# Average pooling over a 537 MB array: loads of 48 KB per partition on one DMA queue and stores of 48 KB on another, in place of 64 KB loads and 32 KB stores on one queue

## The chip, the cores and the metric

The kernel runs on one core of a Trainium2 chip. The core has a VectorE (DVE in the profile), a ScalarE (ACT), a TensorE (PE), a GpSimd (POOL) and a SyncE (SP), an on-chip memory of 128 partitions, and 16 DMA engines that move data between it and the main memory (HBM). DMAs are started by instructions on an engine's instruction stream; those of SP go into SP's DMA queue, those of ACT into ACT's. One DMA over 128 partitions is spread over the 16 engines, eight partitions each.

The metric is the device time of one execution in microseconds, the median of several runs.

## The reference

The input x is 64 x 256 x 8192 in float32; the pooling window and the stride are both 4.

```python
def reference(x: np.ndarray, kernel_size: int, stride: int) -> np.ndarray:
    batch, channels, length = x.shape
    out_len = (length - kernel_size) // stride + 1
    output = np.zeros((batch, channels, out_len), dtype=np.float32)
    for i in range(out_len):
        start = i * stride
        output[:, :, i] = np.mean(x[:, :, start : start + kernel_size], axis=2)
    return output
```

Every four neighbours along the last axis become their mean. Since 8192 is a multiple of 4 and no window crosses a row, the whole array can be read as one flat run of 134,217,728 numbers, each four of which give one output. 536.87 MB are read and 134.22 MB are written.

## The kernel before

The flat array is cut into 32 groups, and a group into 128 contiguous runs of 32,768 numbers (`run`, 128 KB), one for each partition. A group is loaded in two loads (`PER_STORE`), each with 16,384 numbers (`LOAD`, 64 KB) of every partition: 63 full loads, and the last one is cut in two pieces (`LAST`, 11,264 and 5,120 numbers). A tile `xt` holds one load; there are two of them. A tile `ot` holds the results of a whole group, 8,192 numbers (32 KB) per partition; there are two of them as well.

`pool` works on one load. VectorE adds neighbours in pairs, in place (line 51: 16,384 numbers become 8,192), and adds neighbours of the result in pairs into `ot` (line 56: 8,192 become 4,096). ScalarE multiplies these by 0.25 in place (line 57).

All DMAs are issued by SP, in the order of the program: the load of step n (line 70), and behind the second load of a group the store of the group before (line 74). A load waits until VectorE has read the tile that it overwrites, that is until line 56 of step n-2 is done; the store waits for line 57 of its group's second load. So the DMA queue holds load, load, store, load, load, store, one after the other. At the end, behind the two pieces of the last load, stand the store of group 30 (line 74), the store of the first half of group 31 (line 76) and one store for each piece (line 81).

Of the kernel before, what the change touches and what calls it, by code (L numbers as in the profile page):

```python
# [1 line left out]

# [4 lines left out]

ADD = mybir.AluOpType.add

LOAD = 16384  # L10
PER_STORE = 2
LAST = (11264, 5120)


@with_exitstack
def kernel(
    ctx: ExitStack,
    tc: tile.TileContext,
    x: bass.AP,
    kernel_size: bass.AP,  # L20
    stride: bass.AP,
    out: bass.AP,
):

    nc = tc.nc
    K = int(kernel_size)
    assert K == 4 and int(stride) == 4 and x.shape[-1] % 4 == 0
    P = nc.NUM_PARTITIONS  # L30
    dt = x.dtype
    inv_k = 1.0 / K

    run = LOAD * PER_STORE
    total = x.shape[0] * x.shape[1] * x.shape[2]
    groups = total // (P * run)
    assert groups * P * run == total and groups >= 2
    xg = x.flatten_outer_dims().rearrange("r l -> (r l)").rearrange("(g p w) -> g p w", p=P, w=run)
    og = out.flatten_outer_dims().rearrange("r l -> (r l)").rearrange(
        "(g p w) -> g p w", p=P, w=run // K  # L40
    )

    pin = ctx.enter_context(tc.tile_pool(name="xin", bufs=2))
    pout = ctx.enter_context(tc.tile_pool(name="res", bufs=2))

    def pool(xt, at, width, ot, to):


        half = width // 2
        four = xt[:, at : at + width].rearrange("p (m k) -> p m k", k=2)  # L50
        nc.vector.tensor_tensor(  # L51
            out=xt[:, at : at + half], in0=four[:, :, 0], in1=four[:, :, 1], op=ADD
        )
        two = xt[:, at : at + half].rearrange("p (m k) -> p m k", k=2)
        o = ot[:, to : to + width // K]
        nc.vector.tensor_tensor(out=o, in0=two[:, :, 0], in1=two[:, :, 1], op=ADD)  # L56
        nc.scalar.mul(o, o, inv_k)  # L57

    tiles = {}
    for n in range(groups * PER_STORE):  # L60
        g, j = divmod(n, PER_STORE)
        last = n == groups * PER_STORE - 1
        if j == 0:
            tiles[g] = pout.tile([P, run // K], dt, name="ot")
        ot = tiles[g]
        xt = pin.tile([P, LOAD], dt)
        spans, at = [], 0
        for w in LAST if last else (LOAD,):
            lo = j * LOAD + at
            nc.sync.dma_start(out=xt[:, at : at + w], in_=xg[g][:, lo : lo + w])  # L70
            spans.append((at, w))
            at += w
        if j == PER_STORE - 1 and g > 0:
            nc.sync.dma_start(out=og[g - 1], in_=tiles.pop(g - 1)[:, :])
        if last:
            nc.sync.dma_start(out=og[g][:, : j * LOAD // K], in_=ot[:, : j * LOAD // K])
        for at, w in spans:
            to = (j * LOAD + at) // K
            pool(xt, at, w, ot, to)
            if last:  # L80
                nc.sync.dma_start(out=og[g][:, to : to + w // K], in_=ot[:, to : to + w // K])


# [1 line left out]
_INS = ['x', 'kernel_size', 'stride']  # L85
_OUTS = [((64, 256, 2048), 'float32')]

_NUMBERS = {'kernel_size': 4, 'stride': 4}


# [26 lines left out]
```

## Time and profile before

| | |
|---|---|
| median of 3 runs (lowest, highest) | 1558.38 us (1558.06, 1558.56) |
| profiled execution: time | 1558.32 us |
| profiled execution: span from the first to the last instruction | 1556.5 us |
| VectorE busy | 839.8 us, 130 instructions |
| ScalarE busy | 232.9 us, 66 instructions |
| one 64 KB load: line 51, line 56, line 57 | 8.69, 4.43 and 3.62 us |
| median from issue to landing, full loads | 35.2 us, 63 of them |
| median from issue to landing, full stores (4096 KB each) | 41.2 us, 31 of them |
| bytes moved, mean rate over the span | 671.12 MB, 431 GB/s |

Times are in microseconds. The profile's page gives the busy time of each engine as a share of the span, the busy share of the DMA engines in 40 slices of the span (a digit 9 means 90% or more), and for each DMA queue its packets, megabytes and the share of the 16 engines' time. The view in order of time has, for each instruction, its start, its duration, engine, line and operation, what it writes and reads, and in square brackets how long the engine sat idle before it and what ended that. The chain of work that ended last follows the end of the program back to its beginning, at each step to what was waited for; here it has start, duration and what ran. The view of waits has, for each waiting instruction and what it waited for, the time in total, how often, and the longest.

### The profile page before, as it was taken

To read this page: it belongs to the slowest core of one execution; us is meant where nothing else is said; L and a number is where in the kernel's file an instruction comes from. 1 tells how busy PE (TensorE), PEld (TensorE's weight loads), DVE (VectorE), ACT (ScalarE), POOL (GpSimd) and SP (SyncE) were. 2 spreads that over 40 slices of the span, in tenths; PEclk is the share of its full clock that TensorE was granted. 3 is DMA by queue.
4 is the path that set the end of the run, shared out by engine and by line. 5 is a ranking of instruction groups with operands and counts; after the bars stand their busy time and mean duration, and the time that the engine had idled before them with its cause. 6 is when DMAs were issued, how large, how long until landed. Compare 5 with 4: busy or idle time off the path is not lost.

```text
span 1556.5 us, 463 instructions
## 1 busy us (share of the span) xinstructions
DVE 839.8 (54%) x130; ACT 232.9 (15%) x66; POOL 0.2 (0%) x4
## 2 busy tenths in 40 slices
DVE  3645645456454564545645556545465454654546
ACT  1101111111111111111111111010110101101011
POOL 0000000000000000000000000000000000000000
DMA  9999999999999999999999999999999999999999
GB/s 416 445 406 431 431 435 440 431 429 433 423 441 433 431 431 425 440 431 431 435 436 435 437 435 435 428 432 435 431 433 440 428 441 436 433 431 425 440 429 389
DMA packets 14259, 671.12 MB, mean 431 GB/s; under 512 B 1584, under 2 KB 1584, under 8 KB 1712
## 3 DMA queue, kind: packets, MB, share of 16 engines
q1 hardware_dynamic: 14256, 671.09, 99.9%
q14 instruction: 3, 0.02, 0.0%
HBM read 536.87 MB, written 134.22 MB: 431 GB/s over the span
## 4 chain that ended last, share of the span: by engine, by line
DMA 72%; DVE 27%; issue 0%; ACT 0%; SPq 0%
DMA xt<-in_x_dram 72%; DVE xt L51 18%; DVE ot L56 9%; ACT ot L57 0%; SPq L70 0%
## 5 line engine op out<-in xcount | busy, mean ns | idle before, releaser
L51 DVE TENSOR_TENSOR xt<-xt 128x8192 f32<-128x8192 f32 (+1 forms) x65 | 556.5, 8561 | 699.9 <-DMA xt<-in_x_dram 699.8
L57 ACT ACTIVATE ot<-ot 128x4096 f32<-128x4096 f32 (+1 forms) x65 | 231.6, 3564 | 1311.2 <-DVE ot L56 1311.2
L56 DVE TENSOR_TENSOR ot<-xt 128x4096 f32<-128x4096 f32 (+1 forms) x65 | 283.4, 4360 | 3.9
L57 ACT ACT_TABLE_LOAD x1 | 1.3, 1283 | 0.7 <-PEq L98 0.7
L98 POOL MEMSET const-bfloat16-1.0<- 128x1 bf16 x1 | 0.1, 101 | 0.0
L98 POOL MEMSET const-uint8-127<- 128x1 uint8 x1 | 0.1, 101 | 0.0
L98 POOL MEMSET const-float32-0.0<- 128x1 f32 x1 | 0.1, 98 | 0.2 <-issue 0.2
L98 POOL MEMSET const-float32-1.0<- 128x1 f32 x1 | 0.1, 98 | 0.0
## 6 DMA issues: line engine op xcount, KB each, us to landing
out_dram<-ot SPq DMA_DIRECT2D x31, 4096.0 KB, 41.2
xt<-in_x_dram SPq DMA_DIRECT2D x1, 5632.0 KB, 29.1
xt<-in_x_dram SPq DMA_DIRECT2D x1, 2560.0 KB, 34.8
out_dram<-ot SPq DMA_DIRECT2D x1, 2048.0 KB, 17.1
out_dram<-ot SPq DMA_DIRECT2D x1, 1408.0 KB, 12.2
xt<-in_x_dram SPq DMA_DIRECT2D x63, 35.2
out_dram<-ot SPq DMA_DIRECT2D x1, 640.0 KB, 10.7
```

The costliest lines, as they stand in the source:

```text
L51: nc.vector.tensor_tensor(out=xt[:, at : at + half], in0=four[:, :, 0], in1=four[:, :, 1], op=ADD)
L56: nc.vector.tensor_tensor(out=o, in0=two[:, :, 0], in1=two[:, :, 1], op=ADD)
L57: nc.scalar.mul(o, o, inv_k)
L98: nc = _bacc.Bacc("TRN2", target_bir_lowering=False, num_devices=1)
```

## The change

- `LOAD` becomes 12,288 numbers (48 KB per partition), `PER_STORE` becomes 4. A group has runs of 49,152 numbers (192 KB) per partition, its result has 12,288 numbers (48 KB) per partition. There are 21 whole groups, and a rest of 16,384 numbers per partition that is loaded in the same two pieces as before, now into two tiles.
- The store of a group is issued by ACT, right behind the group's fourth multiplication, and no longer by SP behind the loads. The store of the last whole group is still issued by SP, behind the two pieces' loads, and so are the two stores of the rest.
- The tiles keep their number: two `xt` (48 KB, before 64 KB) and two `ot` (48 KB, before 32 KB).
- In the new kernel the two additions stand on lines 53 and 58, the multiplication on line 59, the loads on lines 68 and 80, the store on ACT on line 71, and SP's stores on lines 83 and 86. `pool` is the same.

```diff
-LOAD = 16384
-PER_STORE = 2
+LOAD = 12288
+PER_STORE = 4
 LAST = (11264, 5120)
...
-    run = LOAD * PER_STORE
-    total = x.shape[0] * x.shape[1] * x.shape[2]
-    groups = total // (P * run)
...
+    per_partition = x.shape[0] * x.shape[1] * x.shape[2] // P
+    rest = sum(LAST)
+    whole = (per_partition - rest) // (LOAD * PER_STORE)
...
+    def runs(flat, at, width):
+        return flat[P * at : P * (at + width)].rearrange("(p w) -> p w", p=P)
...
-    tiles = {}
-    for n in range(groups * PER_STORE):
-        g, j = divmod(n, PER_STORE)
-        last = n == groups * PER_STORE - 1
-        if j == 0:
-            tiles[g] = pout.tile([P, run // K], dt, name="ot")
-        ot = tiles[g]
+    full = None
+    for g in range(whole):
+        run = LOAD * PER_STORE
+        src, dst = runs(flat_in, g * run, run), runs(flat_out, g * run // K, run // K)
+        ot = pout.tile([P, run // K], dt)
+        for j in range(PER_STORE):
+            xt = pin.tile([P, LOAD], dt)
+            nc.sync.dma_start(out=xt[:, :], in_=src[:, j * LOAD : (j + 1) * LOAD])
+            pool(xt, 0, LOAD, ot, j * LOAD // K)
+        if g < whole - 1:
+            nc.scalar.dma_start(out=dst, in_=ot[:, :])
+        full = dst, ot
+
+    at = whole * LOAD * PER_STORE
+    src, dst = runs(flat_in, at, rest), runs(flat_out, at // K, rest // K)
+    ot = pout.tile([P, LOAD * PER_STORE // K], dt)
+    pieces, lo = [], 0
+    for w in LAST:
         xt = pin.tile([P, LOAD], dt)
-        spans, at = [], 0
-        for w in LAST if last else (LOAD,):
-            lo = j * LOAD + at
-            nc.sync.dma_start(out=xt[:, at : at + w], in_=xg[g][:, lo : lo + w])
-            spans.append((at, w))
-            at += w
-        if j == PER_STORE - 1 and g > 0:
-            nc.sync.dma_start(out=og[g - 1], in_=tiles.pop(g - 1)[:, :])
-        if last:
-            nc.sync.dma_start(out=og[g][:, : j * LOAD // K], in_=ot[:, : j * LOAD // K])
-        for at, w in spans:
-            to = (j * LOAD + at) // K
-            pool(xt, at, w, ot, to)
-            if last:
-                nc.sync.dma_start(out=og[g][:, to : to + w // K], in_=ot[:, to : to + w // K])
+        nc.sync.dma_start(out=xt[:, :w], in_=src[:, lo : lo + w])
+        pieces.append((xt, lo // K, w))
+        lo += w
+    nc.sync.dma_start(out=full[0], in_=full[1][:, :])
+    for xt, to, w in pieces:
+        pool(xt, 0, w, ot, to)
+        nc.sync.dma_start(out=dst[:, to : to + w // K], in_=ot[:, to : to + w // K])
```

More of the change, by code (lines that the diff above doesn't have):

```diff
@@ L32 @@
     inv_k = 1.0 / K
-    run = LOAD * PER_STORE
-    total = x.shape[0] * x.shape[1] * x.shape[2]
-    groups = total // (P * run)
[L37 to L41, printed above, removed]
+    per_partition = x.shape[0] * x.shape[1] * x.shape[2] // P
+    assert per_partition * P == x.shape[0] * x.shape[1] * x.shape[2]
+    rest = sum(LAST)
+    whole = (per_partition - rest) // (LOAD * PER_STORE)
+    assert whole * LOAD * PER_STORE + rest == per_partition and max(LAST) <= LOAD
+    flat_in = x.flatten_outer_dims().rearrange("r l -> (r l)")
+    flat_out = out.flatten_outer_dims().rearrange("r l -> (r l)")
     pin = ctx.enter_context(tc.tile_pool(name="xin", bufs=2))
     pout = ctx.enter_context(tc.tile_pool(name="res", bufs=2))
+    def runs(flat, at, width):
+        return flat[P * at : P * (at + width)].rearrange("(p w) -> p w", p=P)
     def pool(xt, at, width, ot, to):
```

## The prediction

> **What bounds the kernel now.** I read the page's busy times first, then its DMA queues.
>
> ```profile
> span 1556.5 us, 463 instructions
> DVE 839.8 (54%) x130; ACT 232.9 (15%) x66; POOL 0.2 (0%) x4
> DMA  9999999999999999999999999999999999999999
> q1 hardware_dynamic: 14256, 671.09, 99.9%
> ```
>
> The reader is to see that no compute engine is near full (VectorE 54%), and that the 16 DMA engines are occupied for 99.9% of the span by one queue, SP's, which carries all 671.09 MB. The bound is bytes over the rate of the DMA engines; waits and order matter only where they leave a DMA engine empty or slow a packet.
>
> Next comes the order of time, to get that rate by itself. At the start only loads run:
>
> ```profile
> 22.63 8.69 DVE L51 TENSOR_TENSOR xt<-xt 128x8192 f32<-128x8192 f32 x1 [22.63 <-DMA xt<-in_x_dram]
> ...
> 41.96 8.69 DVE L51 TENSOR_TENSOR xt<-xt 128x8192 f32<-128x8192 f32 x1 [6.18 <-DMA xt<-in_x_dram]
> ...
> 61.30 8.69 DVE L51 TENSOR_TENSOR xt<-xt 128x8192 f32<-128x8192 f32 x1 [6.19 <-DMA xt<-in_x_dram]
> ...
> 81.72 8.69 DVE L51 TENSOR_TENSOR xt<-xt 128x8192 f32<-128x8192 f32 x1 [7.27 <-DMA xt<-in_x_dram]
> ```
>
> Line 51 starts when a load has landed, so 41.96 - 22.63 = 19.33 us is one load of 8.389 MB: 433.9 GB/s. The bracket is VectorE's wait: 6.2 of 19.3 us, so it has slack. The fourth landing comes 20.42 us after the third, 1.1 us late: behind that load the queue turns to its first store.
>
> The chain that ended last shows that turn in every period. One period is two loads and a store; its DMA piece runs from the issue of a load to its landing, behind the rest of the store and the other load:
>
> ```profile
> 289.35 35.80 DMA xt<-in_x_dram
> 325.15 0.02 issue
> 325.17 8.70 DVE xt L51
> ...
> 1355.93 35.16 DMA xt<-in_x_dram
> 1391.09 0.02 issue
> 1391.12 8.70 DVE xt L51
> ...
> 1404.29 35.15 DMA xt<-in_x_dram
> ```
>
> A period is 1404.29 - 1355.93 = 48.36 us late in the run (20.97 MB, 433.7 GB/s: the store goes at the rate of the loads), but its DMA piece is up to 0.65 us longer early on. Adding what the pieces have over 35.15 us gives 3.9 us up to 620 us and nothing behind it; with the 1.1 us of the first turn the kernel loses 5.0 us in its first 14 or so load-to-store turns, and next to none in the last 17. The trace's records of single packets (start, duration, bytes) say where: nearly all long packets (up to 3.6 us against 2.418) are the last of a load with a store behind it, on all 16 engines at once. The 16 engines finish the first load within 0.5 us of each other, a load near the middle of the run within 3.1 us; once they are apart, the turn is free.
>
> **The change, part by part.**
>
> *Bytes and packets.* The bytes stay 671.09 MB. In the packet records a packet of 64 KB takes 2.418 us, one of 32 KB 1.213, one of 45,056 bytes 1.665: all fit 8 ns plus bytes at 27.19 GB/s, for loads (rows 128 KB apart in memory) and stores (32 KB apart) alike. So 48 KB packets at 192 KB apart should take 1.816 us, and a load of 6.29 MB 0.75 x 19.33 = 14.50 us. Loads go from 63 of 64 KB plus two pieces to 84 plus the same two pieces, stores from 31 of 32 KB, one of 16 KB and two small ones to 21 of 48 KB and the two small ones. Per engine that is 8 x (84 + 21 - 63 - 31 - 1) = 80 packets more. At 8 ns it is 0.6 us; the landings follow the bytes alone (32 KB rows add 29.0 - 19.3 = 9.7 us, half a 64 KB load), so at least 0. I take 0.5, and 10 more semaphore writes of 9 ns: 0.1.
>
> *VectorE and ScalarE.* Line 53 (was 51) on 128x6144 lies between the rows 128x5632 (6026 ns) and 128x8192 (8692 ns): 6.56 us. Line 58 on 128x3072, between 2816 (3092 ns) and 4096 (4425 ns): 3.36 us. Together 9.98 us with gaps, against 14.50 for a load. Line 59 on 128x3072: 2.76 us (between 2550 and 3616 ns). None lies on the path as long as a load is always queued.
>
> *Is one always queued?* There are two buffers of x, so load n+2 is issued when line 58 has read load n. From issue to first packet is 1.0 us (SP's first at 0.73, first packet at 1.74), from a landing's last packet to line 51 0.4 us. Spare time per load: 14.50 - 9.98 - 1.4 = 3.1 us (before: 19.33 - 13.13 - 1.4 = 4.8). While a store runs beside the loads they take longer, and it grows. So the queue never runs empty on the slowest engine, which sets every landing; were the cover gone, each missing us would cost 84 us in all. I cost it at nothing.
>
> *Stores on ACT.* A store is issued from ACT behind its four multiplications and no longer from SP behind a load. SP loses this wait:
>
> ```profile
> SPq L74 <- ACT ot L57: 101.9, 31, 3.3
> SPq L70 <- DVE ot L56: 817.2, 62, 13.2
> ```
>
> The 101.9 us held up nobody: behind it on SP stood a load whose own wait (the second line) ended later. Its removal is worth 0. On ACT the store waits for line 59 just ahead; behind it is the next multiplication, which waits for VectorE at least 7 us more. A result buffer is written again four loads after its store is issued, 58 us and more; a store of 6.29 MB that shares the engines half and half lasts 29. Cost 0. The tail keeps its form: one 6.29 MB store is queued on SP behind both last pieces (before: 4.19 and 2.10 MB), 14.5 us that cover VectorE's and ScalarE's last 8.7 us from the landing of the last piece. 0.
>
> *Loads and stores at the same time.* This is the unknown. Twenty stores now run beside loads, about 29 us each, 580 us in all. If an engine takes packets from the queues by turns, each store has 8 load-to-store turns per engine: 160 turns and one at the tail, against 31. The rows bound one turn from 0.0 (late) to 1.1 us (the first); the mean of the 31 is 5.0 / 31 = 0.16 us. Below nothing: the two queues could hide each other's 8 ns per packet (20 x 16 x 8 ns = 2.6 us), or more if reading and writing memory overlap. I take 5.0 us in all, as before: what made the turns free was the engines being 3 us apart, about 14 turns brought that about, and the new kernel has 2 x 8 = 16 turns per engine in its first two stores; behind these I take the late rows. The trace is nearest to that: most of its 31 turns come with the engines apart.
>
> The Trainium skill, page "DMA: Bandwidth & Descriptors", section "Issuing engines are not separate DMA queues", says that transfers started by several engines run on the same 16 DMA engines and interleave, so that a second issuing engine saves only issue time. By that rule the second queue changes nothing; by the early rows of this trace (0.16 us a turn) it costs up to 26 us, and no row here shows two queues at once.
>
> *Sum*, against the profiled execution, 1558.3 us with a span of 1556.5 (median of the three runs 1558.4). Before: first packet at 1.7 + 671.09 MB at 433.7 GB/s 1547.2 + slow first packets 0.5 + turns 5.0 + last receipt 1.3 = 1555.7; 0.8 is unaccounted for and kept. After: 1556.5 + 0.5 + 0.1 + 0 = 1557.1, and 1.8 outside the span: 1558.9 us. Without any cost of turns it would be 1553.9.
>
> **The rivals.** *Turns stay dear (slower).* Each engine alternates load and store packets all through a store, and the turn costs the mean row, not the late one: 1553.9 + 161 x 0.16 = 1579.7 us. It decides for slower by 0.2% once a turn costs over (1561.5 - 1553.9) / 161 = 0.047 us. For it: the long packets sit only at turns, and up to 620 us the turns are dear. Against it: no turn costs that once the engines are apart.
>
> *Mixing is faster.* Loads write the on-chip memory and stores read it; if what limits is one direction of the traffic and not the DMA engine as a whole, 580 us of mixed time speed up: at 3%, say, with the turns as before, 17 us, 1541.5; if only the turns vanish, and the 8 ns, 1551.3. Against it: late in the run, with engines 3 us apart, some store while others load, and the period is still bytes over the same rate. The same page, section "Where 436 GB/s comes from", gives a ceiling of 435.2 GB/s for the 16 engines; by it no more than about 5 us could be won, and no run here shows that ceiling passed.
>
> *Starvation (slower).* The spare 3.1 us is used up on some loads, say with 1 us left empty on each of some 40 loads that have no store beside them: 1558.9 + 40 = 1599 us. Against it is the arithmetic above.
>
> *The change does nothing*: stores on ACT fall where the order of packets does not matter and the turn is gone or the same: 1554 to 1559, within the first case.
>
> **How the numbers follow.** A run resolves about 0.2% here, 3.1 us: same is 1555.3 to 1561.5. Forecast (turns free after the first two stores), chance 0.55: 0.45 same, 0.07 slower, 0.03 faster. Turns stay dear, 0.25: 0.23 slower. Mixing faster or turns gone, 0.15: 0.12 faster, 0.03 same. Starvation 0.03, slower. Nothing changed 0.02, same. In all 0.15 faster, 0.52 same, 0.33 slower. The range reaches from 1552.5 (turns and some overhead gone) to 1570 (0.1 us a turn); I leave out some 0.08 on each side. The likeliest case alone spans 1554 to 1563.
>
> **What would show it.** Right: two DMA queues on the page, SP's with 545 MB (all loads and the last three stores) and ACT's with 126, DMA 99% throughout, landings 14.5 us apart without a store beside them and about 29 with one, four loads and a store in 72.5 us. Wrong: a period clearly above 72.5 us late in the run (turns dear, 0.1 us each adds 0.8), one below 72.2 (mixing faster), or stretches with DMA below 95% in the loads without a store (starvation).

## The result and the profile after

The changed kernel takes 1566.4 us in the median of seven runs (1561.3 to 1573.6), the kernel before 1558.4 us in seven runs beside them. The ratio is 1.0049, 95% interval 1.0028 to 1.0071: slower by half a per cent. The new kernel also scatters over 12 us, where the kernel before stays within 1.5. The profiled execution was the longest of the seven, 1573.6 us, so what it loses is some 7 us more than a median run loses.

The page of the changed kernel, its span, busy times and queues (packets, megabytes, share of the 16 engines' time):

```profile
span 1571.8 us, 557 instructions
DVE 846.4 (54%) x172; ACT 237.1 (15%) x87; POOL 0.2 (0%) x4
DMA  9999999999999999999999999999999999999999
q1 hardware_dynamic: 12816, 545.27, 81.1%
q10 hardware_dynamic: 2880, 125.83, 18.5%
```

The work has moved as forecast: 126 MB go through a second queue, no engine has become the bound, and the DMA engines are still busy nearly all the time, 81.1 + 18.5 = 99.6% of the span against 99.9%. Most of the loss is therefore inside the DMA time: packets that take longer. The order of time of the changed kernel shows one period of four loads late in the run (start, duration, engine, line, tiles, idle time before in brackets):

```profile
1032.96 6.56 DVE L53 TENSOR_TENSOR xt<-xt 128x6144 f32<-128x6144 f32 x1 [4.59 <-DMA xt<-in_x_dram]
...
1060.74 6.56 DVE L53 TENSOR_TENSOR xt<-xt 128x6144 f32<-128x6144 f32 x1 [17.77 <-DMA xt<-in_x_dram]
...
1077.08 6.56 DVE L53 TENSOR_TENSOR xt<-xt 128x6144 f32<-128x6144 f32 x1 [6.38 <-DMA xt<-in_x_dram]
...
1091.60 6.56 DVE L53 TENSOR_TENSOR xt<-xt 128x6144 f32<-128x6144 f32 x1 [4.58 <-DMA xt<-in_x_dram]
...
1106.15 6.56 DVE L53 TENSOR_TENSOR xt<-xt 128x6144 f32<-128x6144 f32 x1 [4.59 <-DMA xt<-in_x_dram]
```

A load with no store beside it lands after 14.52 to 14.55 us. The two loads with the store beside them take 27.78 + 16.34 = 44.12 us, where three transfers of 6.29 MB at 14.53 take 43.59. So the store costs 0.53 us more than its bytes here, and 0.46 us in the first period. The 19 whole periods from 75.80 to 1471.69 us are 73.47 us long on average, against 5 x 14.53 = 72.65: 0.82 us a period, 15.5 us in all. By the packet records about four fifths of that are packets that take longer; the rest is time in which single engines stood without a packet, 4.0 us per engine over these periods (0.1 us in the kernel before), about half of it in one period, an outlier:

```profile
734.90 6.56 DVE L53 TENSOR_TENSOR xt<-xt 128x6144 f32<-128x6144 f32 x1 [4.78 <-DMA xt<-in_x_dram]
...
768.12 6.56 DVE L53 TENSOR_TENSOR xt<-xt 128x6144 f32<-128x6144 f32 x1 [23.21 <-DMA xt<-in_x_dram]
```

Here the landing comes after 33.22 us. In the packet records seven store packets take up to 2.5 us each in place of 1.815, 4.1 us together, and most other engines run dry for 0.5 to 2.8 us before the next load reaches them. Without that period the mean loss is 0.60 us a period.

The packet records also show how an engine serves two queues: load, store, load, store, one packet of 48 KB each, and the packets do not overlap. (The records do not name the engine; a packet is taken to follow the one at whose end it starts.) The long ones (up to 3.6 us against 1.815) are loads; apart from the outlier nearly all store packets keep their 1.815 us.

### The profile page after: what moved, and what is told of

The parts are those of the page before. It is cut to its first block, busy times and chain, and to the rows that moved or that the text cites. A ratio compares the mean times of both kernels' runs of the same rounds, so it can differ in the third digit from the quotient of the medians.

```text
span 1571.8 us, 557 instructions
## 1 busy us (share of the span) xinstructions
DVE 846.4 (54%) x172; ACT 237.1 (15%) x87; POOL 0.2 (0%) x4
## 3 DMA queue, kind: packets, MB, share of 16 engines
q1 hardware_dynamic: 12816, 545.27, 81.1%
q10 hardware_dynamic: 2880, 125.83, 18.5%
## 4 chain that ended last, share of the span: by engine, by line
DMA 71%; DVE 27%; issue 0%; ACT 0%; DVEq 0%
DMA xt<-in_x_dram 71%; DVE xt L53 18%; DVE ot L58 9%; ACT ot L59 0%; DVEq L58 0%
## 5 line engine op out<-in xcount | busy, mean ns | idle before, releaser
L53 DVE TENSOR_TENSOR xt<-xt 128x6144 f32<-128x6144 f32 (+1 forms) x86 | 559.8, 6509 | 706.5 <-DMA xt<-in_x_dram 706.5
L59 ACT ACTIVATE ot<-ot 128x3072 f32<-128x3072 f32 (+1 forms) x86 | 235.8, 2742 | 1320.8 <-DVE ot L58 1320.8
L58 DVE TENSOR_TENSOR ot<-xt 128x3072 f32<-128x3072 f32 (+1 forms) x86 | 286.7, 3334 | 4.5 <-DVE xt L53 0.5
## 6 DMA issues: line engine op xcount, KB each, us to landing
xt<-in_x_dram SPq DMA_DIRECT2D x1, 2560.0 KB, 11.2
out_dram<-ot SPq DMA_DIRECT2D x1, 1408.0 KB, 13.5
```

What stands on the lines that cost most here:

```text
L53: nc.vector.tensor_tensor(out=xt[:, at : at + half], in0=four[:, :, 0], in1=four[:, :, 1], op=ADD)
```

## The experiments

Each was timed beside the kernel before on the same chip. A "turn" is the change from load to store packets; how far "apart" the engines are is the time between the first and the last of the 16 to finish a load. "Loss" below is the mean length of a period of loads and their store, less the length that the same bytes have without a turn (loads of 64 KB 19.34 us, of 48 KB 14.53 us, stores in proportion), read from the landings in the order of time.

| kernel | loads, stores, store queue | median us | ratio to before (95%) | loss per period, us |
|---|---|---|---|---|
| before | 64 KB, 32 KB, SP | 1557.7 to 1558.4 | 1 | 0.17 (5.0 in all, none late) |
| changed | 48, 48, ACT | 1566.4 | 1.0049 (1.0028 to 1.0071) | 0.82 (this profile) |
| e1 | 64, 32, ACT | 1569.1 | 1.0078 (1.0066 to 1.0091) | 0.62 |
| e2 | 48, 48, SP | 1564.0 | 1.0042 (1.0029 to 1.0054) | 0.31 |
| e3 | 48, 2 x 24 (one per two loads), ACT | 1564.7 | 1.0047 (1.0033 to 1.0060) | 0.41 |
| e4 | 48, 12 per load, SP | 1561.4 | 1.0022 (1.0012 to 1.0031) | none from 230 us on, but for two periods |
| e5 | before, engines set apart | 1560.1 | 1.0012 (1.0004 to 1.0021) | 0.01 |
| e6 | e2, engines set apart | 1572.3 | 1.0092 (1.0079 to 1.0104) | 0.51 |
| e7 | 48, 24 per two loads, SP | 1559.6 | 1.0010 (1.0001 to 1.0018) | none after 520 us |
| e8 | 48, 4 x 12, SP | 1567.1 | 1.0059 (1.0045 to 1.0072) | 0.35 |
| e9 | 48, 24 per two loads, ACT | 1561.8 | 1.0032 (1.0019 to 1.0044) | 0.1 |
| e10 | before, apart at less cost | 1557.9 | 0.9999 (0.9991 to 1.0008) | none after 400 us, but for one store (0.4) |
| e11 | e1, engines set apart | 1586.7 | 1.0186 (1.0173 to 1.0199) | 0.98 |
| e12 | 64, 2 x 16 (one per load), ACT | 1555.4 | 0.9984 (0.9975 to 0.9993) | 0.03 |

**The two halves of the change, each alone.** Theory A: the second queue costs. Theory B: the sizes cost. e1 is the kernel before with its stores on ACT:

```diff
-        if j == PER_STORE - 1 and g > 0:
-            nc.sync.dma_start(out=og[g - 1], in_=tiles.pop(g - 1)[:, :])
         if last:
+            nc.sync.dma_start(out=og[g - 1], in_=tiles.pop(g - 1)[:, :])
...
+        if j == PER_STORE - 1 and g < groups - 2:
+            nc.scalar.dma_start(out=og[g], in_=tiles.pop(g)[:, :])
```

> Sizes of the kernel before (64 KB loads, 32 KB stores, two loads to a store), but 30 of the 31 full stores go to ACT's queue, right behind their multiplications. Theory A, the second queue is what costs: a four-load period of the changed kernel is about 0.5 us too long whenever a store runs beside the loads, so 30 stores cost 30 x 0.5 = 15 us over the 1553.9 us without turns: about 1569 us. Theory B, the sizes are what costs (48 KB packets, rows 192 KB apart): 1558.4 us as before.

e2 is the changed kernel with its stores back on SP, behind the second load of the next group:

```diff
             nc.sync.dma_start(out=xt[:, :], in_=src[:, j * LOAD : (j + 1) * LOAD])
+            if j == 1 and full is not None:
+                nc.sync.dma_start(out=full[0], in_=full[1][:, :])
...
-        if g < whole - 1:
-            nc.scalar.dma_start(out=dst, in_=ot[:, :])
```

> Sizes of the changed kernel (48 KB loads and stores, four loads to a store), but every store on SP's queue behind the second load of the next group. Theory A (second queue): 20 turns in one queue, dear only while the 16 engines are aligned: 1555 to 1560 us, periods of four loads and a store at 72.6 us late in the run. Theory B (sizes): about 1566 us as in the changed kernel.

e1 took 1569.1 us as A said, e2 1564.0 and not 1555 to 1560. Each half costs by itself, and they do not add up: 11.2 and 6.1 us alone, 8.0 together. e1 late in the run, in the order of time:

```profile
1089.42 8.69 DVE L51 TENSOR_TENSOR xt<-xt 128x8192 f32<-128x8192 f32 x1 [6.20 <-DMA xt<-in_x_dram]
...
1119.43 8.69 DVE L51 TENSOR_TENSOR xt<-xt 128x8192 f32<-128x8192 f32 x1 [16.80 <-DMA xt<-in_x_dram]
...
1138.74 8.69 DVE L51 TENSOR_TENSOR xt<-xt 128x8192 f32<-128x8192 f32 x1 [6.16 <-DMA xt<-in_x_dram]
```

A period is 1138.74 - 1089.42 = 49.32 us here, where the kernel before has 48.36 at the same place. e2, the same view:

```profile
1097.55 6.56 DVE L53 TENSOR_TENSOR xt<-xt 128x6144 f32<-128x6144 f32 x1 [4.58 <-DMA xt<-in_x_dram]
...
1112.43 6.56 DVE L53 TENSOR_TENSOR xt<-xt 128x6144 f32<-128x6144 f32 x1 [4.87 <-DMA xt<-in_x_dram]
...
1141.40 6.56 DVE L53 TENSOR_TENSOR xt<-xt 128x6144 f32<-128x6144 f32 x1 [19.02 <-DMA xt<-in_x_dram]
```

The load ahead of the store lands after 14.88 us, 0.35 late, although all is in one queue and 1,100 us have passed. In the kernel before this had ended by 620 us. How far apart the engines are differs between the two: in the kernel before it grows from 0.5 to 3.1 us, in e2 it stops at 1.5 to 2.2 us. In e1 it reaches 2.9 to 3.5 us in the loads without a store, from 560 us on, as far as in the kernel before, and yet its periods go on losing some 0.6 us.

**Is being apart the cause?** e5 sets the engines apart from the start, with extra loads into a tile that nobody reads:

```diff
+        if n == 1:
+            for k, p0 in ((12, 0), (8, 16), (5, 32), (3, 40), (1, 48)):
+                nc.sync.dma_start(out=skew[p0 : p0 + k, :], in_=xg[0][p0 : p0 + k, :3328])
```

> The kernel before, with five small extra loads behind the second load, into a tile that nobody reads, on 12, 8, 5, 3 and 1 partitions of 13 KB each: the DMA engines get 0 to 5 extra rows of 0.5 us, so they stand up to 2.5 us further apart from the first turn on. If a turn is dear because the engines turn together, the early DMA pieces of the chain come near 35.15 us from the start, the 5 us of early turns shrink to 1 or 2, and with 2.5 us of extra work on the busiest engine the time is 1555 to 1558 us. If the early turns are dear for another reason (memory addresses, time since the start), 1558.4 + 2.5 = about 1561 us.

The chain that ended last, of e5 (start, duration, what):

```profile
55.95 31.21 DMA xt<-in_x_dram
...
100.36 35.15 DMA xt<-in_x_dram
...
148.72 35.15 DMA xt<-in_x_dram
```

The DMA pieces are at 35.15 us from the second period on, where the kernel before had 35.24, 35.53 and 35.56 us at about the same places. The extra loads put them 3.1 us apart at once. So in one queue, with 32 KB stores, being apart frees the turn; neither the addresses nor the time since the start make it dear. The total is 1560.1 us because the extra loads cost 6.7 us (the second and the third load land 20.28 and 25.06 us after the one ahead, 6.7 us more than two loads take): their 13 KB packets took 1.2 us on average, most about 1.4, in place of 0.5, and a full packet behind each of them up to 3.4 us longer. e10 has extra loads of 10 KB, with rows read from different groups and written to every fourth partition:

```diff
+            for i, k in enumerate((8, 6, 4, 2, 1)):
+                nc.sync.dma_start(
+                    out=skew[(0, 1, 2, 3, 32)[i] : (0, 1, 2, 3, 32)[i] + 4 * k : 4, :], in_=xg[2 + i][0 : 8 * k : 8, :2560]
+                )
```

> The kernel before with five small extra loads behind the second load on 8, 6, 4, 2 and 1 partitions of 10 KB (0.38 us a row), each engine writing its own partitions: up to 1.9 us between the engines. The earlier extra loads cost 6.7 us, more than the 5 us of turns that they removed. If these cost only their 1.9 us and the early turns go to 1 or 2 us: 1556 to 1558 us, at or a little below the kernel before. If short loads on few partitions cost more than their bytes again: 1559 us and up.

It came out at 1557.9 us, the same as before. Its 21 extra packets took 0.385 us each and held up nothing. The engines are 1.8 us apart after them, each dear turn takes them further, and from 400 us on, 3.7 us apart, the turns are free but for one; the 1.9 us of extra packets on the busiest engine eat up what that saves. Applied to e2, the extra loads of e5 give e6:

> The 48 KB sizes with every store on SP's queue (1564.0 us), with the same five extra loads. There the engines never get further apart than about 2.1 us and a turn costs 0.1 to 0.5 us to the end. If being apart is what makes a turn free, 1558 to 1561 us (7 us of turns gone, 2.5 us of extra work), as long as they stay apart. If they draw together again or a turn into 48 KB store packets costs anyway: 1564 to 1567 us.

1572.3 us. The first turn, and one late in the run, in the order of time:

```profile
82.40 6.56 DVE L55 TENSOR_TENSOR xt<-xt 128x6144 f32<-128x6144 f32 x1 [4.65 <-DMA xt<-in_x_dram]
...
98.37 6.56 DVE L55 TENSOR_TENSOR xt<-xt 128x6144 f32<-128x6144 f32 x1 [6.01 <-DMA xt<-in_x_dram]
...
1035.00 6.56 DVE L55 TENSOR_TENSOR xt<-xt 128x6144 f32<-128x6144 f32 x1 [4.58 <-DMA xt<-in_x_dram]
...
1049.88 6.56 DVE L55 TENSOR_TENSOR xt<-xt 128x6144 f32<-128x6144 f32 x1 [4.87 <-DMA xt<-in_x_dram]
```

The extra loads put the engines 3.6 us apart, but with 48 KB stores they do not stay there: they are 2.5 to 2.9 us apart at the first two turns, 2.0 us behind the third, and 1.5 to 2.6 us from then on. The first three turns cost 0.9 to 1.4 us (98.37 - 82.40 = 15.97 against 14.53), more than e2's at the same places (0.97, 0.07 and 0.02); the later ones mostly 0.1 to 0.5 us to the end. So setting the engines apart once frees nothing here; a turn with the engines held 3 us apart is not among its rows. e11 puts the same loads into e1:

> The sizes of the kernel before with 30 stores on ACT's queue (1569.1 us), with the five extra loads of 13 KB behind the second load, which set the DMA engines apart at a cost of 6.7 us. If being apart frees the turns between two queues as it does in one queue: 1553.9 + 6.7 = about 1561 us. If a store that begins on a second queue reaches all engines at once and costs its 0.5 us however far they stand apart: 1569.1 + 5 to 7 = 1574 to 1576 us.

1586.7 us, worse than either theory said: on the second queue being apart does not free the turn, it makes it dearer, 0.98 us a period against 0.62, with the engines 3.2 to 4.5 us apart in the loads without a store to the end:

```profile
1053.35 8.69 DVE L52 TENSOR_TENSOR xt<-xt 128x8192 f32<-128x8192 f32 x1 [6.20 <-DMA xt<-in_x_dram]
...
1083.73 8.69 DVE L52 TENSOR_TENSOR xt<-xt 128x8192 f32<-128x8192 f32 x1 [17.17 <-DMA xt<-in_x_dram]
...
1103.08 8.69 DVE L52 TENSOR_TENSOR xt<-xt 128x8192 f32<-128x8192 f32 x1 [6.19 <-DMA xt<-in_x_dram]
```

That is 49.73 us for a period of 48.36. The step of the prediction that carried the rule of one queue over to two is refuted by this run.

**Does the size of the store packets matter?** In one queue: e7 is e2 with `PER_STORE = 2`, e4 stores after every load, e8 cuts e2's store into four.

```diff
-                nc.sync.dma_start(out=full[0], in_=full[1][:, :])
+                for h in range(0, run // K, LOAD // K):
+                    nc.sync.dma_start(
+                        out=full[0][:, h : h + LOAD // K], in_=full[1][:, h : h + LOAD // K]
+                    )
```

> 48 KB loads with two loads to a store (24 KB per partition), all on SP's queue: 42 turns, about 168 packets per engine more than with 48 KB stores (1.3 us at 8 ns). If the dear turns of the 48 KB sizes come from the size of the store packets (as long as a load packet), they become free after some 14 turns as before: 1557 to 1561 us. If they come from the 48 KB loads: twice the turns of 0.3 us, about 1570 us.

> 48 KB loads, and one store of 12 KB per partition for each load, all on SP's queue: 84 load-to-store turns of all engines in one queue, and 1.7 us of extra packet overhead at most (252 packets more per engine against the changed kernel's stores divided by the 8 ns, bounded by what the landings show). If a turn costs wherever it is (0.07 us each or more): 1562 us and up. If turns in one queue are free once the engines are apart: 1557 to 1560 us.

> 48 KB loads, four loads to a store, all on SP's queue, the store cut into four of 12 KB per partition, one right behind the other: 20 turns as with the 48 KB sizes, but short store packets. 480 packets per engine more than with the 48 KB stores, 3.8 us at 8 ns. If the size of the store packets keeps the turns dear: 7 us less and 3.8 us more than 1564.0, about 1561 us, and the four-load periods lose nothing late in the run. If the number of loads between two turns or the rows 192 KB apart keep them dear: about 1568 us, and the periods lose 0.1 to 0.5 us each.

e7 took 1559.6 us: its turns lose 3.3 us up to 520 us and nothing later. e7, the order of time:

```profile
1081.38 6.56 DVE L53 TENSOR_TENSOR xt<-xt 128x6144 f32<-128x6144 f32 x1 [4.51 <-DMA xt<-in_x_dram]
...
1103.17 6.56 DVE L53 TENSOR_TENSOR xt<-xt 128x6144 f32<-128x6144 f32 x1 [11.84 <-DMA xt<-in_x_dram]
...
1117.69 6.56 DVE L53 TENSOR_TENSOR xt<-xt 128x6144 f32<-128x6144 f32 x1 [4.51 <-DMA xt<-in_x_dram]
```

36.31 us a period. So 48 KB loads are not what keeps turns dear. Nor are rows 192 KB apart: e4 has them, and its four loads with four 12 KB stores take 72.62 us from 230 us on, but for two periods. (Its expectation counted the packets wrongly: they are 504 more per engine than in the changed kernel, 4 us at 8 ns.) In e8 the load ahead of the store lands after 14.53 to 14.6 us in most periods, so its turn is all but free with 20 turns and four loads between them; but the store then takes 0.3 us longer than its bytes, 0.2 of it in 24 more packets at 8 ns, and the time got worse, 1567.1 us. e8 late in the run:

```profile
1025.24 6.56 DVE L53 TENSOR_TENSOR xt<-xt 128x6144 f32<-128x6144 f32 x1 [4.59 <-DMA xt<-in_x_dram]
...
1039.77 6.56 DVE L53 TENSOR_TENSOR xt<-xt 128x6144 f32<-128x6144 f32 x1 [4.52 <-DMA xt<-in_x_dram]
...
1069.16 6.56 DVE L53 TENSOR_TENSOR xt<-xt 128x6144 f32<-128x6144 f32 x1 [19.45 <-DMA xt<-in_x_dram]
```

e8's engines are only 1.4 to 2.0 us apart late in the run, like e2's, so there it is the size of the store packets that makes the turn cheap, and not the distance. In one queue, then, a turn into 48 KB packets stays dear, and one into 12, 24 or 32 KB packets becomes free or nearly so.

On the second queue: e3 cuts the changed kernel's store into two halves, e9 is the changed kernel with `PER_STORE = 2`, and e12 cuts e1's store into two:

```diff
-            nc.scalar.dma_start(out=og[g], in_=tiles.pop(g)[:, :])
+            half, whole = run // K // 2, tiles.pop(g)
+            for h in (0, half):
+                nc.scalar.dma_start(out=og[g][:, h : h + half], in_=whole[:, h : h + half])
```

> The changed kernel, each store on ACT cut into two of 24 KB per partition, one behind the other: 16 store packets per engine and store instead of 8, so twice the turns. If every turn between the queues costs (12 us over 20 x 8 turns), 24 us: about 1578 us. If the cost is paid once, when a store begins beside the loads, or by the bytes stored: about 1566 us, as the changed kernel.

> The changed kernel with two loads to a store: 41 stores of 24 KB per partition on ACT's queue instead of 20 of 48 KB. If a store costs about 0.5 us when it begins on the second queue, whatever its size, 41 x 0.5 = 20 us over 1553.9 + about 2.5 for 160 more short packets and 48 KB loads: about 1577 us. If the cost goes with the bytes that are moved beside loads: about 1566 us as the changed kernel.

> 64 KB loads on SP and 30 stores on ACT's queue (1569.1 us), each store cut into two of 16 KB per partition, one behind the other: 240 more packets per engine, 1.9 us at 8 ns, and twice the turns. If the cost on a second queue goes with the size of the store packets, as it does for turns in one queue, most of the 15 us of slow turns goes: 1558 to 1564 us. If it does not depend on their size: 1569.1 + 1.9 = 1571 us; if each turn costs for itself, 1580 us and up.

The halves do not leave one behind the other, as the expectations of e3 and e12 have it: each leaves as soon as its own part is multiplied. In e3 ACT issues one behind the second and one behind the fourth multiplication of a group:

```profile
951.97 2.76 ACT L59 ACTIVATE ot<-ot 128x3072 f32<-128x3072 f32 x1 [18.26 <-DVE ot L58]
954.76 0.34 ACTq L72 DMA_DIRECT2D out_dram<-ot  x1
...
967.30 2.76 ACT L59 ACTIVATE ot<-ot 128x3072 f32<-128x3072 f32 x1 [12.57 <-DVE ot L58]
...
989.30 2.76 ACT L59 ACTIVATE ot<-ot 128x3072 f32<-128x3072 f32 x1 [19.24 <-DVE ot L58]
992.09 0.34 ACTq L72 DMA_DIRECT2D out_dram<-ot  x1
```

So e3 sends the same stores at the same steps as e9 and differs from it, but for the last whole group's store, only in how far apart the rows lie in memory; and e12 sends a store of 16 KB behind every load.

e3 (1564.7 us) has twice the turns of the changed kernel and costs no more, so turns do not each have a price. e9 (1561.8) has twice the stores and costs less, so a store has no fixed price for beginning beside loads either. e12 is the surprise: 1555.4 us in the median of eleven runs, which lie between 1555.3 and 1555.7. It beats the kernel before by 0.16% (0.07 to 0.25%) and the changed one by 11 us. Its order of time and its queues:

```profile
66.47 8.69 DVE L51 TENSOR_TENSOR xt<-xt 128x8192 f32<-128x8192 f32 x1 [11.41 <-DMA xt<-in_x_dram]
...
90.67 8.69 DVE L51 TENSOR_TENSOR xt<-xt 128x8192 f32<-128x8192 f32 x1 [11.05 <-DMA xt<-in_x_dram]
...
114.84 8.69 DVE L51 TENSOR_TENSOR xt<-xt 128x8192 f32<-128x8192 f32 x1 [11.02 <-DMA xt<-in_x_dram]
```

```profile
q1 hardware_dynamic: 9936, 545.26, 81.1%
q10 hardware_dynamic: 8640, 125.83, 18.9%
```

But for one at 526 us (24.9), every load from the fourth on lands after 24.2 us; 114.84 - 66.47 = 48.37 us is the length of the bytes. Two loads are 16 packets per engine and the store is 16 packets, so the engines alternate all the time and no stretch with loads alone is left. They do so while their finishing times are only 0.4 to 1.0 us apart: being apart is not needed here. Its profile has 8,640 packets in the second queue, three times the changed kernel's, and loses nothing to them.

What stays open: e12 has both short store packets and an alternation that never stops, and no run tells the two apart. e9 (24 KB, loads alone half of the time) loses 0.1 us a period, e3 (24 KB, same share) 0.4, so the packet size alone does not order the profiles; the intervals of the two runs' times overlap, and whether the rows' distance or scatter parts them is not shown. The packet records do show where on the second queue the time is lost: in e1 16.9 of the 17.6 us per engine that load packets are too long fall within 6 us of the first store packet of a store (e11 27.2 of 27.9, the changed kernel 9.2 of 13.5), and 0.7 us in the 18 us of alternation behind. The price is paid where a store begins beside loads that ran alone, and in e12 no load runs alone between stores. Nor does a run show why a load packet ahead of a store gets longer, or why engines that are apart do worse on two queues.

## Why the prediction was right and wrong

The time lies in the range (1552.5 to 1570), 7.5 us above the forecast of 1558.9. The case that came true is the first rival, turns that stay dear (chance 0.25), and not the likeliest one (0.55): the time is above the 1555.3 to 1561.5 that were to be "the same", and the sign named for the rival, periods clearly above 72.5 us late in the run, is there (73.19 us from 1032.96 to 1106.15). That the time is inside the range at all is partly luck: the upper part was put in for that rival at 0.1 us a turn, and a price per turn turned out not to be what sets the loss. The floor without any cost of turns, 1553.9 us, leaves 12.5 us for the median run. Step by step:

- *Nothing but the DMA engines is the bound, no queue runs empty on the slowest engine, the wait that SP loses is worth nothing*: right in the main. VectorE's two steps took 9.95 us a load (9.98 forecast) and its wait in loads without a store was 4.58 us. But the faster engines did run dry now and then, 4.0 us per engine over the 19 periods of the profiled run, a cost that the sum did not have.
- *Bytes and packets, +0.6 us*: too small. A 48 KB load lands after 14.53 us and not after 14.50, so 31.46 MB take 72.65 us, 433.0 GB/s against 433.7; e7, whose late turns are free, runs at 15.73 MB in 36.31 us, 433.2 GB/s. Over 671 MB the former is some 2.5 us, 2 more than the sum had; 8 ns for each of 80 packets does not account for it.
- *The tail, 0*: wrong by 2 us. From the start of line 53 on the first last piece to the end it took 1571.8 - 1543.51 = 28.3 us, before 1556.5 - 1530.17 = 26.3. The tail's bytes did not change, but its last load now turns into a 48 KB store: its 20 KB packets took 0.91 us on average against 0.76, 1.2 us per engine; the other 0.8 us is not accounted for. That store is on SP, and e2 has the same tail (1562.1 - 1533.94 = 28.2). The prediction put the tail at 0 by what covers VectorE, and had its turn only as one of 161.
- *Turns, 5.0 us in all, as before*: the step that failed, in both of its halves. I took the late rows behind the first two stores, since 16 turns would bring the engines 3 us apart and turns are free then. Behind the second store they were 1.0 us apart in a load without a store, behind the fourth 1.9, and later mostly 1.6 to 2.4. And being 3 us apart would not have helped: e1 got there, and its periods went on losing some 0.6 us, e11's 0.98. With 2 us more for the packets and 2 for the tail, the median run lost about 8.5 us beside its 20 stores, 0.4 us each, and the profiled one 15.5. Per turn that is 8.5 / 160 = 0.05 us, at the rival's point of decision of 0.047 and a third of its price of 0.16. But e3 and e9 show that a price per turn is the wrong measure. (The long packets in the profile before were also not on all 16 engines at each dear turn: on 6 to 16 of them, on all 16 at four turns.)
- *The sizes cost nothing but packets*: wrong. e2 shows 6.1 us for the sizes on one queue. Its span is 5.6 us longer than before: 1.9 in the tail, 1.3 in turns (6.3 us in all against 5.0, since the turn into 48 KB packets never becomes free), and the rest, about 2.4, goes with the packets. The late rows of the profile before were for 32 KB store packets, and I carried them over without saying that the store's packet would be half as long again.
- *Being apart makes a turn free*: right for the kernel before (e5), wrong for the two queues (e11), which is where it was used.
- *Mixing is faster*: not in the changed kernel. In e12 it is, by 2.6 us, and to within 1.5 us of the floor: turns gone, but no more than that. Nothing ran faster than one direction alone.
- The Trainium skill's rule that a second issuing engine saves only issue time (page "DMA: Bandwidth & Descriptors", section "Issuing engines are not separate DMA queues") held for where the transfers run: the engines alternate between the queues. It did not hold for the time: the second queue was worth +11.2 us alone, in e1, and -2.6 us with 16 KB stores, in e12.

## What to carry to other kernels

In a kernel that is bound by its DMA engines, as this one is, the order in which an engine meets loads and stores can still have a price, and it hardly shows as idle time: read landing-to-landing times, one stretch with a store and one without, and compare both with the bytes. A price that was read in one queue and for one packet size is not to be carried to another queue or size without a run. Here the two best orders were stores of 32 KB at the back of the load queue, and stores of 16 KB on a second queue that last just as long as the loads beside them; 48 KB stores were dear in either.

## What the runs showed that was not expected

- Two queues are served packet by packet, even where a packet is 48 KB or 64 KB: load, store, load, store on each engine, one at a time.
- On the second queue the price is paid at the start of a store, within some 6 us of its first packet, and hardly at all in the alternation that follows (e1, e11).
- 16 KB store packets that alternate with 64 KB load packets without a break cost nothing, with the 16 engines only 0.4 to 1.0 us apart; 32 KB ones that come in bursts cost 0.6 us a burst, and 0.98 with the engines further apart (e12, e1, e11).
- A few short loads on few partitions can be dear: five with 29 rows of 13 KB, of one group and on neighbouring partitions, took 1.2 us a row in place of 0.5 and held up the full packets behind them by up to 3.4 us, 6.7 us in all (e5). It is not their shortness alone: e10's 21 rows of 10 KB, from different groups and to every fourth partition, took their 0.385 us. Which of these differences counts is not shown.
- How far the runs of a kernel lie from each other differs with the order of its transfers: 12 us for the changed kernel and 6 for e1, but 0.5 us for e12, which uses the same two queues.
